# GpSimd's order in the local-attention stage of a hybrid decoder block: gate-weight sums ahead of the softmax denominators, in an order set by hand

## The chip, the cores and the metric

The kernel runs on one core of one Trainium2 chip. The metric is the device time of one execution in microseconds (us), the median of several runs; lower is better.

## What is computed

One residual block of a decoder with two attention mixers side by side and a SwiGLU, on 1024 tokens of width 1024, all in float32. The part that matters here:

```python
h = rmsnorm(x, mix_norm_g[l])
proj = h @ w_in[l]
qa, ka, va, q_lat, kv_lat, k_r, g_a, g_b = jnp.split(proj, IN_OFFSETS, axis=-1)
...
o_a = swa_sink_attention(qa, ka, va, swa_sinks[l])     # 8 heads, 2 kv heads, window 128
...
o_b = mla_attention(q_nope, q_rope, k_nope, k_rope, vb)
y = jax.nn.sigmoid(g_a) * (o_a @ w_o_swa[l]) + jax.nn.sigmoid(g_b) * (o_b @ w_o_mla[l])
x = x + y @ w_out[l]
h = rmsnorm(x, ffn_norm_g[l])
x = x + (jax.nn.silu(h @ w_gate[l]) * (h @ w_up[l])) @ w_down[l]
```

and in the local attention, per block of 128 queries against 256 keys:

```python
m = jnp.maximum(jnp.max(s, axis=-1, keepdims=True), sink)
p = jnp.exp(s - m)
denom = jnp.sum(p, axis=-1, keepdims=True) + jnp.exp(sink - m)
p = (p / denom).astype(v.dtype)
o = jnp.einsum('bnhgqk,bnkhd->bnqhgd', p, vw)
```

## The kernel before

Every float32 product is made of three products of halves: `split` (L159) lets ScalarE cast an operand to its upper half (L163) and VectorE subtract that from it for the lower half (L166); `mm3` (L168) multiplies upper by upper (L172), upper by lower (L173) and lower by upper (L174).

The stage around the change computes two independent things at once.

*The gate projections*, h @ [g_a | g_b], are most of TensorE's work. They go in eight column groups j, and each group is made of seven block products instead of eight (`Seven`), numbered q and run in the order 1, 6, 2, 7, 5, 4, 3. One `gate_step` (L850) runs one block product, twelve matmuls of 128x512. `run` (L789) first prepares the operand of the step two ahead (`prep`, L764), which means a split of a weight block `wr`, or of a sum `sm` for q = 6 and 5. The sums of the next group are made by `mix` (L750) when the step with q = 5 runs. On GpSimd these are six operations of 128x256, three for each half of the columns: sm0 = a21 + a22 (L180), sm1 = sm0 - a11 (L177) and a21 = a11 - a21 (L177). The weights have been scaled by the norm's gain on ScalarE before (L837). For q = 7 `prep` also subtracts sm1 from a12 in place, two GpSimd operations (L774, in the profile L177 wr<-wr,sm), after the split of a12 for q = 2 has read it.

*Local attention* goes in 16 iterations `it`, each one group of four heads and one block of 128 queries. Iteration `it` of the loop (L1025) issues, in this order: the load of queries two ahead (`sw_q`), gate step 3*it, the transposes of the next queries (`sw_qT`, L896), gate step 3*it+1, the product of probabilities and values of the iteration before (`sw_pv`), the scores of the next iteration (`sw_scores`, L905), gate step 3*it+2, and the transposes of its own probabilities (`sw_pT`, L950). Inside `sw_scores`, VectorE adds the band mask and takes row maxima (L921), joins them with the sinks (nm, L925; es, L927); ScalarE takes the exponentials and their row sums (pe, den, L933); GpSimd adds the sink's term (L935), takes the reciprocal as a power of -1 (L936) and scales the four heads' probabilities (L938).

With seven block products to a group and three steps to an iteration, the place of the sums moves through the loop: they fall to the steps 4, 11, 18, 25, 32, 39 and 46, and the subtractions from a12 to the steps 1, 8, 15, 22, 29, 36, 43 and 50.

What sets the order: TensorE and SyncE (SP, which issues all the DMAs here) run in the order in which the code is written (L335). ScalarE, VectorE and GpSimd are put in order by the framework's scheduler in this stage, since their hand-set stretch (L504) ends before the loop. Each engine works through its list strictly in that order, and waits at an instruction whose inputs aren't there. Tiles of the pools `U` (21 buffers), `V`, and `tiny` (8 buffers of each width) rotate, so an instruction that writes a new tile also waits for the last reader of the buffer's former one.

Of the kernel before, what the change touches and what calls it, by code (L numbers as in the profile page):

```python
# [12 lines left out]
ALU = mybir.AluOpType  # L13
# [76 lines left out]
def hybrid_block_kernel(  # L90
# [29 lines left out]
    nc = tc.nc  # L120
# [23 lines left out]
    def U(name, dt=F32, shape=(P, 1024)):  # L144
        return pool.tile(list(shape), dt, tag="u", name=uid(name))
# [4 lines left out]
    def tiny(name, w=1):  # L150
        return small.tile([P, w], F32, tag=f"t{w}", name=uid(name))

    def P1(name, shape=(P, 512)):
        return ps1.tile(list(shape), F32, tag="ps", name=uid(name))

    def PX(name, shape=(P, 512)):
        return psum["x"].tile(list(shape), F32, tag="ps", name=uid(name))
# [24 lines left out]
    def blk(b, n=1):  # L182
        return slice(b * P, (b + n) * P)
# [10 lines left out]
    neg_one = const.tile([P, 4], F32, name="neg_one")  # L194
# [139 lines left out]
    engines = mybir.EngineType  # L334
# [486 lines left out]
    sw = {}  # L821
# [28 lines left out]
    def gate_step():  # L850
        late = gate_stores[:]
        gate_stores.clear()
        gates.run()
        for d, t in late:
            nc.sync.dma_start(d, t)
# [3 lines left out]
    def sw_q(it):  # L859
        qn = U("qn")  # L860
        nc.sync.dma_start(qn[:, 0:256], q_d[it])
        sw[it] = {"qn": qn}
# [28 lines left out]
    def sw_qT(it):  # L891
        d = sw[it]
        qn = d.pop("qn")
        ptq = PX("qT", (P, 2, P))
        for j in range(2):
            nc.tensor.transpose(ptq[:, j], qn[:, blk(j)], ident)  # L896
        qs = U("qs", F32R, (P, 2, 2, P))
        e, o = qs[:, :, 0], qs[:, :, 1]
        nc.scalar.copy(e[0:64], ptq[0:64])
        nc.scalar.copy(o[64:128], ptq[64:128])  # L900
        nc.vector.tensor_tensor(e[64:128], ptq[0:64], e[0:64].bitcast(F32), op=ALU.subtract)
        nc.vector.tensor_tensor(o[0:64], ptq[64:128], o[64:128].bitcast(F32), op=ALU.subtract)
        d["qs"] = qs

    def sw_scores(it):  # L905
        g, b = divmod(it, NB)
        d = sw[it]
        qs = d.pop("qs")
        c0 = P if b == 0 else 0
        kc = slice((b - 1) * P + c0, (b + 1) * P)  # L910
        mx = tiny("mx", 4)
        scs = []
        for hp in range(2):
            sc = PX("sc", (P, 2, 2 * P))
            scs.append(sc)
            for j in range(2):
                nc.tensor.matmul(sc[:, j, c0:], qs[:, hp, j], khd[g][0][:, kc], start=True, stop=False)
                nc.tensor.matmul(sc[:, j, c0:], qs[:, hp, j], khd[g][1][:, kc], start=False, stop=True)
            for j in range(2):
                h = 2 * hp + j  # L920
                nc.vector.tensor_tensor_reduce(sc[:, j, c0:], sc[:, j, c0:], band[:, c0:], 1.0, NEG, op0=ALU.add,  # L921
                                               op1=ALU.max, accum_out=mx[:, h:h + 1])
        ns = nsink[:, 4 * g:4 * g + 4]
        nm = tiny("nm", 4)
        nc.vector.scalar_tensor_tensor(nm, mx, -SC_A, ns, op0=ALU.mult, op1=ALU.min)  # L925
        es = tiny("es", 4)
        nc.vector.tensor_tensor(es, nm, ns, op=ALU.subtract)  # L927
        den = tiny("den", 4)
        pe = U("pe", F32, (P, 4, 2 * P))
        for h in range(4):  # L930
            if h == 1:
                nc.scalar.activation(es, es, AF.Exp)
            nc.scalar.activation(pe[:, h, c0:], scs[h // 2][:, h % 2, c0:], AF.Exp, scale=SC_A, bias=nm[:, h:h + 1],  # L933
                                 accum_out=den[:, h:h + 1])
        nc.gpsimd.tensor_tensor(den, den, es, op=ALU.add)  # L935
        nc.gpsimd.tensor_tensor(den, den, neg_one, op=ALU.pow)  # L936
        for h in range(4):
            nc.gpsimd.tensor_scalar(pe[:, h, c0:], pe[:, h, c0:], den[:, h:h + 1], 0.0, op0=ALU.mult, op1=ALU.add)  # L938
        d["pe"] = pe
        d["kbs"] = [1] if b == 0 else [0, 1]  # L940

    def sw_pT(it):
        d = sw[it]
        pe = d.pop("pe")
        d["pth"] = U("pth", F32R, (P, 2, 4, P))
        d["ptl"] = U("ptl", F32R, (P, 2, 4, P))
        for kb in d["kbs"]:
            pp = P1("pT", (P, 4, P))
            for h in range(4):
                nc.tensor.transpose(pp[:, h], pe[:, h, blk(kb)], ident)  # L950
            split(d["pth"][:, kb], d["ptl"][:, kb], pp)

    def sw_pv(it):
        g, b = divmod(it, NB)
        d = sw.pop(it)
        kbs = d["kbs"]
        po = P1("o", (P, 2, 2, P))
        for kb in kbs:
            kblk = b - 1 + kb
            vst = vv[kblk // 4][:, kblk % 4, g]  # L960
            nc.tensor.matmul(po, vst, d["pth"][:, kb], start=kb == kbs[0], stop=False)
            nc.tensor.matmul(po, vst, d["ptl"][:, kb], start=False, stop=kb == 1)
        tmp = U("ot", F32, (P, 2, 2, P))
        nc.scalar.copy(tmp[0:64], po[64:128])
        if b % 4 == 0:
            oa_t[it // 4] = U("oa", F32, (P, 2, 512))
        oa = oa_t[it // 4]
        oc = blk(b % 4)
        nc.vector.tensor_tensor(oa[0:64, :, oc], po[0:64, :, 0], tmp[0:64, :, 0], op=ALU.add)
        nc.vector.tensor_tensor(oa[64:128, :, oc], po[0:64, :, 1], tmp[0:64, :, 1], op=ALU.add)  # L970
        if b % 4 == 3:
            nc.sync.dma_start(oa_d[it // 4], oa_t.pop(it // 4))
# [6 lines left out]
    for i, b in enumerate((4, 5, 6, 7, 0, 1, 2, 3)):  # L979
        ps = P1("kl", (P, KVL))  # L980
        mm3(ps, [(hT(k, blk(b)), (wkl[k // 4][0][:, k % 4], wkl[k // 4][1][:, k % 4])) for k in range(NK)])
        t = U("lat", F32, (P, 2, KVL))
        nc.scalar.copy(t[:, 0], ps)
        ss = tiny("ss")
        nc.scalar.activation(t[:, 1], t[:, 0], AF.Square, accum_out=ss)
        r = rstd_of(ss, KVL)
        if i == 0:
            latent_end(NB - 1)
            sw_qT(0)
            while lat_out:  # L990
                lat_store()
        if i == 2:
            gates.prep_to(1)
        if i == 3:
            gates.mix(0, nc.vector)
        if i == 4:
            sw_scores(0)
            gates.prep_to(2)
        if i >= 4:
            t4_of_h(i - 4)  # L1000
        scaled.append((t, r, b))
        if i == 4:
            gates.load_part(1, 0)
        while len(scaled) > (2 if i < 5 else 1):
            kv_out(*scaled.pop(0))
# [12 lines left out]
    def load_lat(n):  # L1018
        for b in range(len(lat), n):
            t = U("lat", F32, (P, LAT))  # L1020
            nc.sync.dma_start(t, lat_d[b])
            lat.append(t)

    N_SW = 2 * NB
    for it in range(N_SW):  # L1025
        if it + 2 < N_SW:
            sw_q(it + 2)
        gate_step()
        if it + 1 < N_SW:
            sw_qT(it + 1)  # L1030
        gate_step()
        if it >= 1:
            sw_pv(it - 1)
        if it + 1 < N_SW:
            sw_scores(it + 1)
        if it == N_SW - 1:
            load_lat(4)
        gate_step()
        sw_pT(it)
    gate_step()  # L1040
    gate_step()
    sw_pv(N_SW - 1)
    in_order.__exit__(None, None, None)


# [314 lines left out]
    for t in range(NT):  # L1360
        h, n = divmod(t, NB)
# [16 lines left out]
        if t in fill:  # L1378
            dc, sh, c0 = fill[t]
# [505 lines left out]
```

## Time and profile before

| | us |
|---|---|
| median of 3 runs | 1340.86 |
| lowest and highest | 1339.17, 1341.85 |
| the profiled execution | 1340.2 |
| its span in the trace | 1338.4 |
| TensorE busy | 1325.0 |
| VectorE busy | 904.0 |
| ScalarE busy | 635.5 |
| GpSimd busy | 566.9 |

Local attention and most of the gate projections lie between about 128 and 330 us. In the profile's rows an instruction is named by engine (PE is TensorE, DVE VectorE, ACT ScalarE, POOL GpSimd), the line of the kernel, the operation, and the tiles that it writes and reads (out<-in). A timeline row begins with its start and its duration; "x4" means four like it in a row, and brackets hold the engine's idle time just before and what ended it. `wl` is a prepared weight operand, `pT` the transposes of probabilities, `qT` those of queries.

### The profile page before, as it was taken

Reading aid. Unit: us, or ns where it says so; the run is one execution under the profiler, and the core shown is the slowest. Engines: PE = TensorE matmul, PEld = TensorE weight load, DVE = VectorE, ACT = ScalarE, POOL = GpSimd, SP = SyncE. Lnnn points to the kernel's source line nnn. Section 1 sums busy time; section 2 is a strip of 40 time slices with the busy share of each in tenths; the row PEclk is TensorE's granted clock in tenths of the full one; section 3 lists DMA queues with packets and bytes.
Section 4 is the critical chain, followed back from the end, with each engine's and each line's share of the span. In section 5 each row is a group of like instructions: output and inputs, shape, how many; then the busy total and the mean of one; then the engine's idle time right before and its main releaser. Section 6 shows DMA issues by size and latency. Waiting matters only on the chain. (4 is left out here: it accounts for less than half of the span.)

```text
span 1338.4 us, 19037 instructions
## 1 busy us (share of the span) xinstructions
PE 1325.0 (99%) x6564; PEld 1115.5 (83%) x6564; DVE 904.0 (68%) x1471; ACT 635.5 (47%) x1291; POOL 566.9 (42%) x614
## 2 busy tenths in 40 slices
PE   9999999999999999999999999999999999999997
PEld 6899878888888889888887888888888888888886
DVE  7868777776767766696468766566655564664862
ACT  7434767665557666763436323222233232644443
POOL 2116546553224555451131765756666541022521
PEclk9999999999999999999999999999999999999999
DMA  9455332245476440681533344535543425996504
GB/s 370 158 184 160 114 104 84 100 134 178 161 235 174 95 111 17 240 281 61 212 139 104 144 173 171 198 143 182 181 147 144 170 100 193 386 367 238 173 15 143
DMA packets 85311, 223.61 MB, mean 167 GB/s; under 512 B 9632, under 2 KB 16288, under 8 KB 84128
## 3 DMA queue, kind: packets, MB, share of 16 engines
q1 hardware_dynamic: 83776, 220.05, 47.9%
q10 hardware_dynamic: 1440, 2.36, 0.5%
q8 instruction: 52, 0.85, 0.3%
q14 instruction: 43, 0.35, 0.1%
HBM read 151.72 MB, written 70.12 MB: 166 GB/s over the span
## 5 line engine op out<-in xcount | busy, mean ns | idle before, releaser
L166 DVE TENSOR_TENSOR wl<-wr,wl 128x512 fp32r<-128x512 f32 x150 | 149.3, 1019 | 72.0 <-ACT wl L163 71.7
L166 DVE TENSOR_TENSOR lrv<-lr,lrv 128x1024 fp32r<-128x1024 f32 x77 | 105.2, 1397 | 48.7 <-ACT lrv L163 44.6
L163 ACT CAST lrv<-lr 128x1024 fp32r<-128x1024 f32 x77 | 80.0, 1052 | 95.0 <-PE fd L174 70.1
L172 PE MATMUL fd<-lrv 128*128 128x512 f32 x308 | 119.8, 389 | 0.0
L173 PE MATMUL fd<-lrv 128*128 128x512 f32 x308 | 119.8, 389 | 0.0
L174 PE MATMUL fd<-lrv 128*128 128x512 f32 x308 | 119.8, 389 | 0.0
L177 POOL TENSOR_TENSOR wr<-wr,sm 128x512 f32<-128x512 f32 (+1 forms) x38 | 46.6, 1234 | 145.8 <-DVE wl L166 115.5
L163 ACT CAST wl<-wr 128x512 fp32r<-128x512 f32 x150 | 87.0, 623 | 1.8 <-DVE wr L835 1.5
L1198 POOL TENSOR_TENSOR denb<-denb,neg_one 128x1 f32<-128x1 f32 x64 | 40.1, 626 | 96.2 <-ACT p L1197 84.0
L166 DVE TENSOR_TENSOR wl<-sm,wl 128x512 fp32r<-128x512 f32 x60 | 49.0, 844 | 46.4 <-ACT wl L163 46.2
L173 PEld LDWEIGHTS fd<-lrv 128*128 128x128 f32 x308 | 57.8, 188 | 12.1
L172 PEld LDWEIGHTS fd<-lrv 128*128 128x128 f32 x308 | 57.8, 188 | 12.0
L174 PEld LDWEIGHTS fd<-lrv 128*128 128x128 f32 x308 | 57.8, 188 | 11.8
L311 POOL TENSOR_SCALAR ms<-ss 128x1 f32<-128x1 f32 x32 | 8.5, 266 | 138.1 <-ACT xn L1644 61.0
L1197 ACT ACTIVATE p<-scb,nmb 128x384 f32<-128x384 f32 (+3 forms) x64 | 47.8, 747 | 33.3 <-DVE nmb L1196 25.6
L166 DVE TENSOR_TENSOR ptl<-pTb,pth 128x512 fp32r<-128x512 f32 (+2 forms) x96 | 50.5, 552 | 16.6 <-ACT pth L163 16.3
L1196 DVE CUSTOM_DVE_ANT_0 scb<-scb,mask 128x384 f32<-128x384 f32 (+3 forms) x64 | 48.6, 762 | 15.0 <-PE scb L1188 13.0
L1529 ACT ACTIVATE act<-sm 128x512 f32<-128x512 f32 x11 | 7.0, 634 | 104.4 <-DVE sm L180 104.4
L1199 POOL TENSOR_SCALAR p<-p,denb 128x384 f32<-128x384 f32 (+3 forms) x64 | 47.9, 748 | 6.3
L1529 ACT ACTIVATE act<-pu 128x512 f32<-128x512 f32 x22 | 13.9, 633 | 70.8 <-DVE pu L180 70.8
L163 ACT CAST pth<-pTb 128x512 fp32r<-128x512 f32 (+2 forms) x96 | 43.4, 482 | 8.5 <-PE pTb L1213 7.5
L172 PE MATMUL fb<-t2h,wl 128*128 128x512 f32 x120 | 47.4, 395 | 0.0
(356 smaller groups left out, 4318.0 us busy)
## 6 DMA issues: line engine op xcount, KB each, us to landing
lr<-la_d SPq DMA_DIRECT2D x77, 256.0 KB, 5.4
wr<-in_w_gate_dram SPq DMA_DIRECT2D x22, 512.0 KB, 4.2
wr<-in_w_up_dram SPq DMA_DIRECT2D x22, 512.0 KB, 5.2
wd<-in_w_down_dram SPq DMA_DIRECT2D x22, 512.0 KB, 7.2
rb_d<-wd SPq DMA_DIRECT2D x22, 512.0 KB, 2.7
la_d<-sd SPq DMA_DIRECT2D x22, 512.0 KB, 5.7
lr<-rb_d SPq DMA_DIRECT2D x44, 256.0 KB, 5.4
lr<-in_w_down_dram SPq DMA_DIRECT2D x33, 256.0 KB, 5.2
```

What stands on the lines that cost most here:

```text
L163: i = nc.scalar.copy(hi, src)
L166: (eng or nc.vector).tensor_tensor(lo, src, hi.bitcast(F32), op=ALU.subtract)
L172: nc.tensor.matmul(ps, ah, bh, start=first and i == 0, stop=False, skip_group_check=go_on)
L173: nc.tensor.matmul(ps, ah, bl, start=False, stop=False, skip_group_check=go_on)
L174: nc.tensor.matmul(ps, al, bh, start=False, stop=last and i == n - 1, skip_group_check=go_on)
L177: eng.tensor_tensor(out, a, b, op=ALU.subtract)
L311: nc.gpsimd.tensor_scalar(ms, ss, 1.0 / width, EPS, op0=ALU.mult, op1=ALU.add)
L1196: nc.vector.tensor_tensor_reduce(s_, s_, m_, 1.0, -NEG, op0=ALU.add, op1=ALU.min, accum_out=nm)
L1197: nc.scalar.activation(p_, s_, AF.Exp, scale=-1.0, bias=nm, accum_out=den)
L1198: nc.gpsimd.tensor_tensor(den, den, neg_one[:, 0:1], op=ALU.pow)
L1199: nc.gpsimd.tensor_scalar(p[:, 0:w], p[:, 0:w], den, 0.0, op0=ALU.mult, op1=ALU.add)
L1529: nc.scalar.activation(dst, src, AF.Silu)
```

## The change

The two operations on denominators and the four scalings move out of `sw_scores` into a function `norm`, which the loop calls one iteration later in the program: for iteration `it` behind gate step 3*it and the transposes of the next queries. Around the loop GpSimd is put into the order in which the code is written.

```diff
-        nc.gpsimd.tensor_tensor(den, den, es, op=ALU.add)
-        nc.gpsimd.tensor_tensor(den, den, neg_one, op=ALU.pow)
-        for h in range(4):
-            nc.gpsimd.tensor_scalar(pe[:, h, c0:], pe[:, h, c0:], den[:, h:h + 1], 0.0, op0=ALU.mult, op1=ALU.add)
+
+        def norm():
+            nc.gpsimd.tensor_tensor(den, den, es, op=ALU.add)
+            nc.gpsimd.tensor_tensor(den, den, neg_one, op=ALU.pow)
+            for h in range(4):
+                nc.gpsimd.tensor_scalar(pe[:, h, c0:], pe[:, h, c0:], den[:, h:h + 1], 0.0, op0=ALU.mult, op1=ALU.add)
+
+        d["norm"] = norm
...
+    pool_order = tc.manual_schedule(engines={engines.Pool})
+    pool_order.__enter__()
     for it in range(N_SW):
         if it + 2 < N_SW:
             sw_q(it + 2)
         gate_step()
         if it + 1 < N_SW:
             sw_qT(it + 1)
+        sw[it].pop("norm")()
         gate_step()
...
     sw_pv(N_SW - 1)
+    pool_order.__exit__(None, None, None)
     in_order.__exit__(None, None, None)
```

In the built programs TensorE, VectorE, ScalarE and SyncE have their instructions in the same order as before; only GpSimd's list differs, and in iterations 4 to 6 and 11 to 13 alone, apart from the order of the six sums among themselves. Six of ScalarE's instructions (L933) and seven of VectorE's (mostly L927 and L969) get an explicit wait for GpSimd that was implied before by another one.

GpSimd's list at iteration 4, before the change. `den_2201` and `pe_2202` are that iteration's denominators and probabilities, `sm_2217` the sums of gate group 2 and `wr_2025`, `wr_2089` its weights:

```order
L938 TENSOR_SCALAR pe_2072<-pe_2072,den_2071 128x256 x4
L180 TENSOR_TENSOR sm_2217<-wr_2025,wr_2089 128x256
L935 TENSOR_TENSOR den_2201<-den_2201,es_2199 128x4
L180 TENSOR_TENSOR sm_2217<-wr_2025,wr_2089 128x256
L936 TENSOR_TENSOR den_2201<-den_2201,neg_one 128x4
L177 TENSOR_TENSOR sm_2217<-sm_2217,wr_2025 128x256
L938 TENSOR_SCALAR pe_2202<-pe_2202,den_2201 128x256 x4
L177 TENSOR_TENSOR wr_2025<-wr_2025 128x2x128
L177 TENSOR_TENSOR sm_2217<-sm_2217,wr_2025 128x256
L177 TENSOR_TENSOR wr_2025<-wr_2025 128x2x128
```

The same place on GpSimd with the change, where the numbers of the tiles and the lines differ (`den_2203`, `pe_2204`, `sm_2213`, `wr_2027`, `wr_2085`; L937 to L940 stand for L935 to L938):

```order
L940 TENSOR_SCALAR pe_2074<-pe_2074,den_2073 128x256 x4
L180 TENSOR_TENSOR sm_2213<-wr_2027,wr_2085 128x256
L177 TENSOR_TENSOR sm_2213<-sm_2213,wr_2027 128x256
L177 TENSOR_TENSOR wr_2027<-wr_2027 128x2x128
L180 TENSOR_TENSOR sm_2213<-wr_2027,wr_2085 128x256
L177 TENSOR_TENSOR sm_2213<-sm_2213,wr_2027 128x256
L177 TENSOR_TENSOR wr_2027<-wr_2027 128x2x128
L937 TENSOR_TENSOR den_2203<-den_2203,es_2201 128x4
L938 TENSOR_TENSOR den_2203<-den_2203,neg_one 128x4
L940 TENSOR_SCALAR pe_2204<-pe_2204,den_2203 128x256 x4
```

The denominators and scalings stood among the six sums and now stand behind them. Iteration 11 reads alike.

GpSimd's list at iterations 5 and 6, before the change. `den_2328` and `den_2459` are the denominators of these iterations, `wr_2089` (subtracting `sm_2217`) is the pair for a12 of gate group 2, and `sm_2514` are the sums of group 3:

```order
L935 TENSOR_TENSOR den_2328<-den_2328,es_2326 128x4
L936 TENSOR_TENSOR den_2328<-den_2328,neg_one 128x4
L938 TENSOR_SCALAR pe_2329<-pe_2329,den_2328 128x256 x4
L177 TENSOR_TENSOR wr_2089<-wr_2089,sm_2217 128x2x128 x2
L935 TENSOR_TENSOR den_2459<-den_2459,es_2457 128x4
L936 TENSOR_TENSOR den_2459<-den_2459,neg_one 128x4
L938 TENSOR_SCALAR pe_2460<-pe_2460,den_2459 128x256 x4
L180 TENSOR_TENSOR sm_2514<-wr_2344,wr_2385 128x256 x2
L177 TENSOR_TENSOR sm_2514<-sm_2514,wr_2344 128x256
```

The same place on GpSimd with the change (`den_2330`, `den_2461`, `wr_2085` and `sm_2510` are the same tiles under new numbers):

```order
L177 TENSOR_TENSOR wr_2085<-wr_2085,sm_2213 128x2x128 x2
L937 TENSOR_TENSOR den_2330<-den_2330,es_2328 128x4
L938 TENSOR_TENSOR den_2330<-den_2330,neg_one 128x4
L940 TENSOR_SCALAR pe_2331<-pe_2331,den_2330 128x256 x4
L180 TENSOR_TENSOR sm_2510<-wr_2340,wr_2381 128x256
L177 TENSOR_TENSOR sm_2510<-sm_2510,wr_2340 128x256
L177 TENSOR_TENSOR wr_2340<-wr_2340 128x2x128
L180 TENSOR_TENSOR sm_2510<-wr_2340,wr_2381 128x256
L177 TENSOR_TENSOR sm_2510<-sm_2510,wr_2340 128x256
L177 TENSOR_TENSOR wr_2340<-wr_2340 128x2x128
L937 TENSOR_TENSOR den_2461<-den_2461,es_2459 128x4
```

The pair for a12 moved ahead of iteration 5's denominators, and the six sums ahead of iteration 6's. Iterations 12 and 13 read alike.

## The prediction

> **What bounds the kernel now.** I read the page first. Its first part says which engine is full:
>
> ```profile
> PE 1325.0 (99%) x6564; PEld 1115.5 (83%) x6564; DVE 904.0 (68%) x1471; ACT 635.5 (47%) x1291; POOL 566.9 (42%) x614
> ```
>
> TensorE (PE) is busy for 1325.0 of 1338.4 us, so nothing that is done on GpSimd (POOL) counts unless TensorE stands still for it. The next view is therefore what TensorE itself waited for, cut to the stretch in which local attention runs (128 to 330 us), and then the timeline of its probability transposes (pT), one group per iteration:
>
> ```profile
> PE fa L172 <- ACT wl L163: 1.9, 2, 1.1
> ...
> 181.33 1.03 PE L950 MATMUL pT<-ident,pe 128*128 128x128 f32 x8
> 192.54 1.03 PE L950 MATMUL pT<-ident,pe 128*128 128x128 f32 x8
> 205.49 1.03 PE L950 MATMUL pT<-ident,pe 128*128 128x128 f32 x8
> ...
> 271.89 1.03 PE L950 MATMUL pT<-ident,pe 128*128 128x128 f32 x8
> 284.53 1.03 PE L950 MATMUL pT<-ident,pe 128*128 128x128 f32 x8
> ```
>
> The first row says that TensorE waited twice here, 1.9 us in all, each time for a ScalarE (ACT) cast of gate weights. The start times give the full price. From 181.33 to 192.54 is 11.21 us, an undisturbed iteration. From 192.54 to 205.49 is 12.95, and from 271.89 to 284.53 is 12.64, for the same work. These are the intervals behind iterations 4 and 11 of 0 to 15. The losses are 1.74 and 1.43 us, **3.17 us together**. They exceed the 1.9 us because TensorE also restarts slowly:
>
> ```profile
> 196.15 0.38 PE L896 MATMUL qT<-ident,qn 128*128 128x128 f32 x2
> ...
> 197.61 0.50 PE L172 MATMUL fa<-hh,wl 128*128 128x512 f32 x1 [1.08 <-ACT wl L163]
> ...
> 198.34 0.50 PE L174 MATMUL fa<-hh,wl 128*128 128x512 f32 x1
> 198.67 0.40 PE L172 MATMUL fa<-hh,wl 128*128 128x512 f32 x1
> 198.91 0.40 PE L173 MATMUL fa<-hl,wl 128*128 128x512 f32 x1
> ```
>
> The three products that start from 197.61 took until 198.67, 1.06 us, where the next one took 0.24 (198.67 to 198.91). The third (L174) multiplies by the lower half of the weights, which comes from VectorE (DVE) after the cast.
>
> Who made that cast late is read backwards, first on ScalarE, then VectorE, then GpSimd. The figure in brackets is the idle time before a row and what ended it.
>
> ```profile
> 175.70 1.71 ACT L837 ACTIVATE wr<-wr,gT 128x256 f32<-128x256 f32 x4
> 190.25 0.62 ACT L163 CAST wl<-sm 128x512 fp32r<-128x512 f32 x1 [4.10 <-POOL sm L177]
> 195.03 0.48 ACT L933 ACTIVATE pe<-sc,nm 128x256 f32<-128x256 f32 x1 [3.67 <-DVE nm L925]
> 196.93 0.63 ACT L163 CAST wl<-wr 128x512 fp32r<-128x512 f32 x1
> ...
> 188.19 0.43 DVE L902 TENSOR_TENSOR qs<-qT,qs 64x256 fp32r<-64x256 f32 x1
> 190.91 0.69 DVE L166 TENSOR_TENSOR wl<-sm,wl 128x512 fp32r<-128x512 f32 x1 [2.29 <-ACT wl L163]
> 195.03 0.16 DVE L927 TENSOR_TENSOR es<-nm,nsink 128x4 f32<-128x4 f32 x1
> 197.59 0.69 DVE L166 TENSOR_TENSOR wl<-wr,wl 128x512 fp32r<-128x512 f32 x1 [1.80 <-ACT wl L163]
> ...
> 176.69 0.74 POOL L180 TENSOR_TENSOR sm<-wr,wr 128x256 f32<-128x256 f32 x1 [0.95 <-ACT wr L837]
> 183.53 0.20 POOL L935 TENSOR_TENSOR den<-den,es 128x4 f32<-128x4 f32 x1 [6.10 <-ACT pe L933]
> 183.68 0.74 POOL L180 TENSOR_TENSOR sm<-wr,wr 128x256 f32<-128x256 f32 x1
> 185.82 0.74 POOL L177 TENSOR_TENSOR sm<-sm,wr 128x256 f32<-128x256 f32 x1
> 186.54 2.27 POOL L938 TENSOR_SCALAR pe<-pe,den 128x256 f32<-128x256 f32 x4
> 189.48 0.74 POOL L177 TENSOR_TENSOR sm<-sm,wr 128x256 f32<-128x256 f32 x1
> ...
> 269.31 0.62 ACT L163 CAST wl<-sm 128x512 fp32r<-128x512 f32 x1 [3.81 <-POOL sm L177]
> ```
>
> The late cast is wl<-wr at 196.93. It stands on ScalarE behind the exponentials, which began at 195.03 after 3.67 us of waiting for VectorE; VectorE was late because wl<-sm at 190.91 came late; and that waited for ScalarE's cast of the sums at 190.25, which had waited 4.10 us for GpSimd. GpSimd had begun the six sums at 176.69, but its second operation was the denominators of iteration 4 (183.53), for which it sat idle 6.10 us, and the last sum that is needed ran at 189.48, behind the four scalings at 186.54. Iteration 11 repeats this: 3.81 us before 269.31. So the wait that TensorE pays at 197.61 begins 14 us earlier, with one GpSimd instruction (183.53) that stands ahead of the sums and isn't ready.
>
> **The change part by part.** No work is added or removed: 16 times two operations on denominators and four scalings, seven times six sums, eight pairs of subtractions, as before. What moves is order on one engine. It issues no DMA, and SP, ScalarE, VectorE and TensorE keep their order.
>
> *Iterations 4 and 11: sums ahead.* The inputs of the sums are scaled by ScalarE at 175.70 to 177.41, all four pieces. From 176.69 six sums of 0.74 us end at about 181.1, before the exponentials of iteration 4 let the denominators start at 183.53. The denominators lose nothing. The cast of the sums can go when ScalarE is free, 190.25-4.10 = 186.15. VectorE is free at 188.62 (188.19+0.43) instead of waiting to 190.91, so its chain from there to es at 195.03 moves up by 2.29 us; the exponentials begin at 192.74, the critical cast runs 194.64 to 195.27, its lower half 195.30 to 195.99. TensorE comes for the upper half behind qT, at 196.15+0.38 = 196.53 at the latest, and for the lower half two products (0.46) later. Both are there about 1 us early (195.27 for 196.53, 195.99 for 196.99). Gain 1.74 us, and 1.43 us in iteration 11: **3.17 us**.
>
> *Iterations 5 and 12: the subtraction from a12 (two operations) ahead of the denominators. Iterations 6 and 13: six sums ahead.* These rows show what is queued behind, and when TensorE comes for it:
>
> ```profile
> 197.13 0.20 POOL L935 TENSOR_TENSOR den<-den,es 128x4 f32<-128x4 f32 x1 [6.21 <-ACT pe L933]
> 198.52 1.84 POOL L938 TENSOR_SCALAR pe<-pe,den 128x256 f32<-128x256 f32 x4
> 200.32 1.86 POOL L177 TENSOR_TENSOR wr<-wr,sm 128x256 f32<-128x256 f32 x2
> 207.75 0.20 POOL L935 TENSOR_TENSOR den<-den,es 128x4 f32<-128x4 f32 x1 [5.56 <-ACT pe L933]
> 209.14 2.37 POOL L938 TENSOR_SCALAR pe<-pe,den 128x256 f32<-128x256 f32 x4
> ...
> 203.06 1.71 ACT L837 ACTIVATE wr<-wr,gT 128x256 f32<-128x256 f32 x4
> ...
> 216.70 1.03 PE L950 MATMUL pT<-ident,pe 128*128 128x128 f32 x8
> ```
>
> The pair (200.32, 1.86 us) must wait for VectorE's lower half of the same weights, by the above 196.0, so it runs to 197.9; denominators and scalings (1.39 us from 197.13 to 198.52, then 1.84 to 2.37) end near 201.6, where they ended at 200.36. TensorE transposes them at 205.49-1.74 = 203.75: 2.1 us to spare. The sums of iteration 6 wait for the scaled weights of 203.06 to 204.77, some 2 us earlier now, and for the scalings; they end near 206.6, the denominators follow to 210.4, and TensorE comes at 216.70-1.74 = 214.96. Cost nothing; if the cover were gone, each us beyond it would be a us of TensorE, and the transposes stand ahead of all later gate products in its queue.
>
> *New waits.* Six first exponentials on ScalarE and seven VectorE instructions (es, oa, one wl) now wait for GpSimd by name, because a rotated buffer was last read there. What they name are denominators and scalings two iterations back, and an iteration is 11.21 us. Behind each stands its engine's whole queue, but at that age the price is nothing.
>
> *What the trace doesn't show* is sums running while VectorE makes the row maxima final. GpSimd was always waiting then. Now sums overlap nm and es (the maxima's sign and the sinks, both short) in iterations 6 and 13, and reach up to them in 4 and 11. Nearest rows:
>
> ```profile
> 184.00 0.97 DVE L166 TENSOR_TENSOR wl<-wr,wl 128x512 fp32r<-128x512 f32 x1 [1.78 <-ACT wl L163]
> 208.21 0.69 DVE L166 TENSOR_TENSOR wl<-wr,wl 128x512 fp32r<-128x512 f32 x1 [1.76 <-ACT wl L163]
> 205.45 0.16 DVE L925 SCALAR_TENSOR_TENSOR nm<-mx,nsink 128x4 f32<-128x4 f32 x1
> ...
> 209.23 0.48 PE L172 MATMUL fb<-t4h,wl 128*128 128x512 f32 x1
> ```
>
> The subtraction that makes a lower half took 0.97 us beside a GpSimd sum (184.00) and 0.69 without one (208.21): such an overlap costs 0.3 us. For nm and es the bounds are nothing and one sum each, 2 x 0.74 = 1.48 us. The lower half ends at 208.90 and is wanted two products (0.46) behind 209.23, at 209.69, so 0.8 us are free: a loss of 0 to 0.7 us per place, 0 to 1.4 in all. A gain is excluded, since GpSimd was idle beside them. I take nothing, since 2 x 0.3 us, by the nearest row, fits into the 0.8.
>
> [...]
>
> *Carrying it to the end.* Time saved in mid-kernel is only kept if TensorE stays the bound. These two windows (bounds, length, then TensorE busy) say it does:
>
> ```profile
> 330.00:390.00 60.00, 60.00 (x281) 49.59 (x280) 38.19 (x65) 28.13 (x54) 12.44 (x12) 1.00 0.63 211
> 722.00:1115.00 393.00, 393.00 (x1734) 325.49 (x1735) 252.47 (x310) 117.18 (x215) 227.73 (x158) 1.00 0.45 160
> ```
>
> The sum against the profiled execution is 1340.2-3.2 = 1337.0 us. That execution lies 0.7 us under the median of the three runs (1340.86), so the forecast for the median is **1337.7 us**.
>
> **The rivals.** *Both stalls go* (forecast): 1337.7. For it: the sums' inputs are there by 177.41, 6 us before the place that held them.
>
> *The saving is partly taken back*, by sums that delay nm and es in iterations 6 and 13, or because the cast of iterations 4 and 11 turns out tighter than my 1 us. Against it: one overlap was seen to cost 0.3 us. With it, 0.5 to 1.6 us of the 3.2 return (the 1.4 above, and 0.2 for a tighter cast): 1338.2 to 1339.3, at its likeliest 1339. [...]
>
> *The change doesn't do what it says*: ScalarE's late exponentials have another cause, for instance VectorE's own backlog, and both waits remain: 1340.9. Against it: VectorE idled before 190.91, and ScalarE before 190.25, both behind that sum.
>
> *Slower, by late probabilities.* In strict order the subtraction of iterations 5 and 12 holds denominators and scalings behind VectorE. If GpSimd ended them later than 203.75, TensorE would stand at pT, twice. The spare 2.1 us is the point from which it decides. If both old stalls still go, a net loss of 2.7 us needs (3.2+2.7)/2 = 2.9 us beyond that at each place, 5.0 us in all; even a pair of twice its 1.86 us would bring 1.9. It would then be about 1344.
>
> **How the numbers follow.** A measurement of this kernel tells about 0.2%, 2.7 us, from no change, and the forecast gain of 3.2 lies only just beyond it. Chances: both stalls go 0.66, partly back 0.23, no effect 0.06, slower 0.05. The first case lands a little under the bound now and then (0.08), and the second once in ten beyond it, so faster 0.60, same 0.35, slower 0.05. The three runs before lie from 1.7 below their median to 1.0 above it. So the range goes from 1337.7-1.7 = 1336.0 to the partial case's upper bound and the same spread, 1339.3+1.0 = 1340.3; it leaves out no effect and slower.
>
> **What would show it.** Right: iterations 4 and 11 take 11.21 us from pT to pT like the rest, TensorE's wait for the cast of wl is gone between 128 and 330 us, and GpSimd's six sums stand in one run from about 176.7 to 181. The scalings of iteration 5 then end about 2 us before their transposes. Wrong: nm or es longer than 0.16 us in iterations 6 and 13 with a wait of TensorE some 4 us later (partly back); an idle time before pT with GpSimd as releaser (slower); or a wait that moved to another engine ahead of 196.9.

## The result, and the profile after

The changed kernel took 1338.30 us (median of 22 runs, 1336.31 to 1340.04) against 1340.78 us of the kernel before beside it (22 runs). The two medians differ by 2.5 us; the ratio, worked out over all these runs, is 0.9976, which is 3.2 us less, with a 95% interval of 0.9969 to 0.9983, 2.3 to 4.2 us. 1337.7 was predicted, 1336.0 to 1340.3 as the range. The profiled execution took 1336.93 us with a span of 1335.1; the span of before was 1338.4, 3.3 us more.

What TensorE waited for between 128 and 330 us is an empty answer now: the row of the cast (1.9 us, 2 times) is gone and no other has come. TensorE's busy time is the page's first part again; then the starts of the probability transposes, from its timeline:

```profile
PE 1323.6 (99%) x6564; PEld 1115.3 (84%) x6564; DVE 904.6 (68%) x1471; ACT 636.5 (48%) x1291; POOL 567.0 (42%) x614
```

```profile
180.87 1.03 PE L954 MATMUL pT<-ident,pe 128*128 128x128 f32 x8
192.08 1.03 PE L954 MATMUL pT<-ident,pe 128*128 128x128 f32 x8
203.29 1.03 PE L954 MATMUL pT<-ident,pe 128*128 128x128 f32 x8
...
269.69 1.03 PE L954 MATMUL pT<-ident,pe 128*128 128x128 f32 x8
280.91 1.03 PE L954 MATMUL pT<-ident,pe 128*128 128x128 f32 x8
```

192.08 to 203.29 is 11.21 us where 12.95 stood, and 269.69 to 280.91 is 11.22 where 12.64 stood. From the first transposes of the loop to the last, sixteen groups, it is 147.88 to 313.29 = 165.41 us against 148.37 to 316.91 = 168.54: **3.13 us saved**, all of it in these two intervals. The profiled execution also began its loop 0.49 us earlier, ahead of anything that the change touches, so times of the two traces are compared as distances from a transposition and not as they stand.

Behind the next query transposes of iteration 4, the gate products now run without a gap: the first starts at 195.83, and from the second on one follows every 0.23 to 0.24 us:

```profile
195.69 0.38 PE L896 MATMUL qT<-ident,qn 128*128 128x128 f32 x2
195.83 0.48 PE L172 MATMUL fa<-hh,wl 128*128 128x512 f32 x1
196.14 0.40 PE L173 MATMUL fa<-hl,wl 128*128 128x512 f32 x1
196.38 0.40 PE L174 MATMUL fa<-hh,wl 128*128 128x512 f32 x1
196.61 0.40 PE L172 MATMUL fa<-hh,wl 128*128 128x512 f32 x1
```

The chain that led there, in GpSimd's, ScalarE's and VectorE's timelines of the changed kernel:

```profile
176.23 0.74 POOL L180 TENSOR_TENSOR sm<-wr,wr 128x256 f32<-128x256 f32 x1 [0.95 <-ACT wr L837]
...
179.96 0.73 POOL L177 TENSOR_TENSOR wr<-wr 128x256 f32<-128x256 f32 x1
183.19 0.20 POOL L937 TENSOR_TENSOR den<-den,es 128x4 f32<-128x4 f32 x1 [2.50 <-ACT pe L933]
...
195.19 1.44 POOL L177 TENSOR_TENSOR wr<-wr,sm 128x256 f32<-128x256 f32 x2 [8.24 <-DVE wl L166]
196.59 0.20 POOL L937 TENSOR_TENSOR den<-den,es 128x4 f32<-128x4 f32 x1
196.87 1.51 POOL L938 TENSOR_TENSOR den<-den,neg_one 128x4 f32<-128x4 f32 x1
198.47 2.36 POOL L940 TENSOR_SCALAR pe<-pe,den 128x256 f32<-128x256 f32 x4
201.26 0.74 POOL L180 TENSOR_TENSOR sm<-wr,wr 128x256 f32<-128x256 f32 x1 [0.43 <-ACT wr L837]
...
202.77 0.74 POOL L177 TENSOR_TENSOR wr<-wr 128x256 f32<-128x256 f32 x1
203.47 0.73 POOL L180 TENSOR_TENSOR sm<-wr,wr 128x256 f32<-128x256 f32 x1
...
204.97 0.74 POOL L177 TENSOR_TENSOR wr<-wr 128x256 f32<-128x256 f32 x1
205.90 0.20 POOL L937 TENSOR_TENSOR den<-den,es 128x4 f32<-128x4 f32 x1 [0.19 <-ACT pe L933]
...
207.29 2.36 POOL L940 TENSOR_SCALAR pe<-pe,den 128x256 f32<-128x256 f32 x4
```

```profile
185.77 0.62 ACT L163 CAST wl<-sm 128x512 fp32r<-128x512 f32 x1
...
191.84 0.47 ACT L933 ACTIVATE pe<-sc,nm 128x256 f32<-128x256 f32 x1 [2.69 <-DVE nm L925]
...
193.75 0.63 ACT L163 CAST wl<-wr 128x512 fp32r<-128x512 f32 x1
...
203.61 0.47 ACT L933 ACTIVATE pe<-sc,nm 128x256 f32<-128x256 f32 x1 [1.63 <-POOL wr L177]
```

```profile
187.69 0.69 DVE L166 TENSOR_TENSOR wl<-sm,wl 128x512 fp32r<-128x512 f32 x1
...
191.84 0.16 DVE L927 TENSOR_TENSOR es<-nm,nsink 128x4 f32<-128x4 f32 x1
...
194.41 0.69 DVE L166 TENSOR_TENSOR wl<-wr,wl 128x512 fp32r<-128x512 f32 x1 [1.44 <-ACT wl L163]
...
202.86 0.67 DVE L925 SCALAR_TENSOR_TENSOR nm<-mx,nsink 128x4 f32<-128x4 f32 x1
203.56 0.65 DVE L927 TENSOR_TENSOR es<-nm,nsink 128x4 f32<-128x4 f32 x1
...
206.36 0.69 DVE L166 TENSOR_TENSOR wl<-wr,wl 128x512 fp32r<-128x512 f32 x1 [1.55 <-ACT wl L163]
```

The six sums run in one piece from 176.23 to 180.69, and the denominators of iteration 4 still start at 183.19. ScalarE casts the sums at 185.77 with no wait in brackets, VectorE follows at 187.69, its es stands at 191.84 instead of 195.03, and the cast that TensorE had waited for starts at 193.75 instead of 196.93. It ends 1.45 us before the first product that needs it (194.38 for 195.83), and VectorE's lower half 1.28 us before the third (195.10 for 196.38). The scalings of iteration 5 end at 200.83, 2.46 us ahead of 203.29. One thing is new: nm and es of iteration 6 (202.86 and 203.56) took 0.67 and 0.65 us, each while a sum ran on GpSimd. The same two of iteration 13 took 0.67 and 0.58; in the kernel before neither took more than 0.17 anywhere in the loop. In iterations 2, 4 and 11 the last sum now ends inside nm, which took 0.28 to 0.30 there. (The exponential at 203.61 names the sum that ended at 203.51, but it also needs nm, which ended at 203.53; for iteration 13 the profile names nm.)

### The profile page after: what moved, and what is told of

Its sections match the earlier page's. It is cut to its first block, busy times and chain, and to the rows that moved or that the text cites. A ratio compares the mean times of both kernels' runs of the same rounds, so it can differ in the third digit from the quotient of the medians.

```text
span 1335.1 us, 19045 instructions
## 1 busy us (share of the span) xinstructions
PE 1323.6 (99%) x6564; PEld 1115.3 (84%) x6564; DVE 904.6 (68%) x1471; ACT 636.5 (48%) x1291; POOL 567.0 (42%) x614
## 5 line engine op out<-in xcount | busy, mean ns | idle before, releaser
L166 DVE TENSOR_TENSOR wl<-wr,wl 128x512 fp32r<-128x512 f32 x150 | 148.7, 1015 | 71.2 <-ACT wl L163 70.9
L166 DVE TENSOR_TENSOR lrv<-lr,lrv 128x1024 fp32r<-128x1024 f32 x77 | 105.1, 1396 | 49.0 <-ACT lrv L163 46.4
L166 DVE TENSOR_TENSOR wl<-sm,wl 128x512 fp32r<-128x512 f32 x60 | 48.2, 829 | 42.2 <-ACT wl L163 42.1
L172 PEld LDWEIGHTS fd<-lrv 128*128 128x128 f32 x308 | 57.8, 188 | 11.9
L166 DVE TENSOR_TENSOR ptl<-pTb,pth 128x512 fp32r<-128x512 f32 (+2 forms) x96 | 50.5, 551 | 16.6 <-ACT pth L163 16.2
```

The source lines that it names most:

```text
L166: (eng or nc.vector).tensor_tensor(lo, src, hi.bitcast(F32), op=ALU.subtract)
L172: nc.tensor.matmul(ps, ah, bh, start=first and i == 0, stop=False, skip_group_check=go_on)
```

## The experiments

The intervals below are differences of the starts of neighbouring groups of probability transposes, behind the iteration named; all others are 11.2 us in all kernels, save those behind iteration 0 (10.3 to 11.9, ahead of the change's first effect), 8 and 14 (10.3 and 10.0 everywhere). Ratios are to the kernel before, run beside each.

| kernel | behind 4 | 5 | 11 | 12 | ratio (95%) |
|---|---|---|---|---|---|
| before | 12.95 | 11.21 | 12.64 | 11.21 | 1 |
| the change | 11.21 | 11.22 | 11.22 | 11.21 | 0.9976 (0.9969 to 0.9983) |
| only sums ahead in 4, 11 | 11.23 | 11.23 | 11.22 | 11.23 | 0.9973 (0.9964 to 0.9981) |
| sums behind | 13.75 | 11.23 | 13.48 | 11.22 | 1.0017 (1.0008 to 1.0026) |
| all but those sums | 15.19 | 11.21 | 14.93 | 11.22 | 1.0032 (1.0021 to 1.0043) |
| two more powers | 11.21 | 11.22 | 11.21 | 11.21 | 0.9975 (0.9966 to 0.9984) |
| four more powers | 11.80 | 12.30 | 11.80 | 12.34 | 1.0002 (0.9994 to 1.0011) |
| two-input ops beside sums | 11.21 | 11.66 | 11.21 | 11.65 | 0.9984 (0.9975 to 0.9992) |
| two-input ops alone | 11.22 | 11.23 | 11.22 | 11.23 | 0.9978 (0.9969 to 0.9986) |
| one-input ops beside sums | 11.23 | 11.67 | 11.23 | 11.66 | 0.9989 (0.9981 to 0.9998) |

*Which part brings the gain.* The change has three parts that can be had one by one, since a denominator function called at its old place stays ahead of the sums and the pair. The next three kernels differ from the changed one only in that:

```diff
-        d["norm"] = norm
+        if it in (3, 4, 10, 11):
+            d["norm"] = norm
+        else:
+            norm()
...
-        sw[it].pop("norm")()
+        if "norm" in sw[it]:
+            sw[it].pop("norm")()
```

With this condition only the sums of 4 and 11 go ahead:

> Only one part of the change: the sums of iterations 4 and 11 stand ahead of the denominators; the pairs of iterations 5 and 12 and the sums of 6 and 13 stand where they stood before. My theory: the whole gain, 3.2 us below before (ratio 0.9976), 11.21 us from pT to pT in every full iteration; nm and es of iterations 6 and 13 back at 0.16 us each (0.67 and 0.65 in the changed kernel). Rival (the pairs and the later sums carry part of the gain): a gain clearly under 3 us, with an interval over 11.5 us left behind iteration 4, 5, 6, 11, 12 or 13.

It has the whole gain, 0.9973, and every interval at 11.2. nm and es of iteration 6 are short again, in VectorE's timeline of this kernel:

```profile
203.80 0.16 DVE L925 SCALAR_TENSOR_TENSOR nm<-mx,nsink 128x4 f32<-128x4 f32 x1
204.00 0.16 DVE L927 TENSOR_TENSOR es<-nm,nsink 128x4 f32<-128x4 f32 x1
...
206.62 0.69 DVE L166 TENSOR_TENSOR wl<-wr,wl 128x512 fp32r<-128x512 f32 x1 [1.42 <-ACT wl L163]
```

So the other two parts of the change bring nothing. With the condition `it in (3, 10)` GpSimd's order is also set by hand, but the sums of 4 and 11 stand wholly behind:

> GpSimd's order set by hand as in the change, but in iterations 4 and 11 the six sums stand wholly behind the denominators and scalings, and iterations 5, 6, 12, 13 are as before the change. My theory (only the sums' place counts): in the changed kernel the denominators of iteration 4 ran at 183.19 and its scalings ended at 186.95; five sums of 0.74 us behind them end near 190.6, 0.4 us later than the 190.22 of before, so both stalls stay and grow by about 0.4 us each: pT to pT 13.3 and 13.0 us, all told 0.8 us above the kernel before (ratio 1.0006). Rival (an order by hand at all, or the explicit waits, brings the gain): about 3 us below before, ratio 0.998, and 11.21 us from pT to pT throughout.

The stalls stayed and grew, to 2.53 and 2.26 us over 11.22; a hand-set order alone gains nothing. They grew by 0.80 and 0.84, twice what was expected: that estimate set a time of the changed kernel's trace against one of before without taking off the 0.49 us between their starts. TensorE's waits between 128 and 330 us, and the fifth sum on GpSimd with the cast that it releases on ScalarE:

```profile
PE fa L172 <- ACT wl L163: 3.2, 2, 1.6
```

```profile
190.15 0.74 POOL L177 TENSOR_TENSOR sm<-sm,wr 128x256 f32<-128x256 f32 x1
```

```profile
190.92 0.62 ACT L163 CAST wl<-sm 128x512 fp32r<-128x512 f32 x1 [4.89 <-POOL sm L177]
```

The third condition, `it not in (4, 11)`, is the rest of the change without its first part:

> The rest of the change without its first part: the pairs of iterations 5 and 12 ahead of the denominators and the sums of 6 and 13 ahead of theirs, but the sums of 4 and 11 behind. My theory: as with the sums behind and nothing else changed, about 0.8 us above before (ratio 1.0006), pT to pT 13.3 and 13.0 us behind iterations 4 and 11, the rest 11.21. Two places shift against each other here: with the stall back, VectorE's lower half of the pair's weights is late, so the pair and with it the denominators of iteration 5 come about 2 us later, but TensorE comes later by the stall too. Rival (the later parts carry gain): below before by 1 us or more.

No gain, as expected, but 15.19 and 14.93 us instead of 13.3 and 13.0. The wait was no longer than with the sums behind alone (3.2 us in two waits in both). What came on top is in the windows of the trace (bounds, length, busy time of the five engines, then TensorE's granted clock) and in TensorE's timeline:

```profile
198.00:200.00 2.00, 1.35 (x4) 0.84 (x5) 1.37 (x3) 2.00 (x6) 0.60 (x1) 0.92 0.96 347
200.00:203.00 3.00, 3.00 (x8) 2.32 (x8) 2.91 (x6) 2.93 (x8) 2.82 (x5) 0.50 0.46 177
```

```profile
198.65 0.53 PE L172 MATMUL fa<-hh,wl 128*128 128x512 f32 x1 [1.59 <-ACT wl L163]
...
199.75 0.63 PE L172 MATMUL fa<-hh,wl 128*128 128x512 f32 x1
200.18 0.63 PE L173 MATMUL fa<-hl,wl 128*128 128x512 f32 x1
```

After the stall the granted clock was 0.50, and products started 0.43 us apart instead of 0.23, until 203.1. Whether the pairs or the later sums bring this on, or chance, took four more kernels on one chip: sums behind and the pairs of 5 and 12 ahead (`it in (3, 5, 10, 12)`), sums behind and only the later sums ahead (`it in (3, 6, 10, 13)`), and both kernels from above again.

> Sums of iterations 4 and 11 behind the denominators as in the run with the sums behind, and in addition the pairs of 5 and 12 ahead of the denominators as in the change; sums of 6 and 13 behind theirs. That run was at 1.0017 of before with stalls of 2.53 and 2.26 us; with the pairs and the later sums ahead as well it was 1.0032, and after both stalls TensorE's granted clock was 0.50 for some 3.5 us (200 to 203 us), which made each interval 1.44 longer. If the drop of the clock is a matter of chance after a stall of 1.6 us, it comes in some executions of this kernel and of the other three here, whatever GpSimd's order: the same mix of mean clocks from 0.996 to 0.999 and times of about 1342 without a drop, 1343.5 with one, 1345 with two. If the pair ahead brings it on: near 1.0032, clock 0.996 to 0.997 in most runs, unlike the kernel without it.

> Sums of iterations 4 and 11 behind the denominators, pairs of 5 and 12 behind them too, and only the sums of 6 and 13 ahead of theirs. If the drop of the clock is chance: intervals behind iterations 4 and 11 of about 13.7 and 13.5 us, or 1.45 more where a drop falls, and a ratio between 1.0010 and 1.0035 like the others. If the sums of 6 and 13 ahead cost time by themselves (the nm and es held beside them, 1.0 us per place): intervals behind iterations 5, 6, 12 or 13 above 11.3 us, and up to 1.1 us above the run with the sums behind.

> The kernel with the sums behind and nothing else, once more, beside the other three on one chip. Without a drop of the clock, 2.5 and 2.3 us at the two places, against 1.74 and 1.43 before: 1.6 us above before (ratio 1.0012). If the drop is chance, some of its runs have a mean clock of 0.997 or less and are 1.45 us longer per drop, the profiled one perhaps too.

> The kernel with everything but the first part of the change, once more, on the same chip. If the drop is chance, its median moves towards that of the kernel with the sums behind (ratio 1.0012 to 1.0035), and the profiled execution may have none, with intervals of 13.7 and 13.5 us behind iterations 4 and 11. If the order of the pairs and the later sums brings the drop on, it stays at about 1.0032 with two drops in the profile and clocks of 0.996, 1.5 us or more above the kernel with the sums behind.

| kernel | behind 4 | behind 11 | ratio (95%) | runs with a mean clock of 0.996 |
|---|---|---|---|---|
| pairs ahead | 15.17 | 13.34 | 1.0025 (1.0016 to 1.0033) | 3 of 11 |
| later sums ahead | 13.75 | 13.47 | 1.0020 (1.0012 to 1.0029) | 1 of 11 |
| sums behind again | 13.73 | 13.45 | 1.0023 (1.0013 to 1.0032) | 3 of 10 |
| all but those sums again | 13.63 | 13.32 | 1.0020 (1.0011 to 1.0029) | 3 of 11 |

In the six profiles of these kernels here and above, two drops go with a mean clock of 0.996, one with 0.997, and none with 0.998 or 0.999; that is how the last column is read. The four intervals of the ratio overlap. Behind iterations 5, 6, 12 and 13 the kernel with only the later sums ahead shows 11.2 us, so those sums cost nothing by themselves. With the pairs ahead one drop came, behind iteration 4 alone. The kernel with all but those sums had two in its first profile and none in the second, whose window from 200 to 203 us reads:

```profile
200.00:203.00 3.00, 3.00 (x17) 2.54 (x16) 2.91 (x6) 2.94 (x8) 2.82 (x4) 1.00 0.49 195
```

So the order of the pairs doesn't decide it; the drop comes by execution, though 4 of 7 runs at 0.996 against 0 of 11 had suggested otherwise in the first comparison. What brings it on in one execution and not in the next stays open. Over the 61 executions of these kernels there and here, the 14 with a mean clock of 0.996 had a median of 1345.8 us, the 34 with 0.998 or 0.999 one of 1343.1. A drop lengthened its interval by some 1.5 us (15.19 against 13.63 for one kernel, 14.93 against 13.32).

*How much the late scalings may cost.* In iterations 5 and 12 of the changed kernel, more work was put ahead of the scalings, at first two reciprocals:

```diff
+            for _ in range(2 if it in (5, 12) else 0):
+                nc.gpsimd.tensor_tensor(den, den, neg_one, op=ALU.pow)
             nc.gpsimd.tensor_tensor(den, den, neg_one, op=ALU.pow)
```

> The changed kernel with two more reciprocals of the denominators (each undoes the other) on GpSimd in iterations 5 and 12, ahead of the scalings. In the changed kernel the scalings of iteration 5 ended at 200.83 and TensorE began the transposes at 203.29: 2.46 us spare. Two reciprocals of 1.02 us and their gaps are about 2.2 us. My theory (the spare time is a true cushion): 0 to 0.2 us lost per place, the time that of the changed kernel (ratio to before 0.9976 to 0.998), 11.21 us from pT to pT within 0.2. Rival (the wait is tighter than it looks, because queues or write latency take part of the spare time): 1 us or more lost at each place, and TensorE idle before pT.

No loss. GpSimd's last scaling and TensorE's transposes in this kernel:

```profile
201.83 1.84 POOL L942 TENSOR_SCALAR pe<-pe,den 128x256 f32<-128x256 f32 x4
```

```profile
203.94 1.03 PE L956 MATMUL pT<-ident,pe 128*128 128x128 f32 x8
```

The scalings ended at 203.67, 0.27 us ahead of 203.94. With `range(4 ...)` instead:

> The changed kernel with four more reciprocals of the denominators (in pairs that undo each other) on GpSimd in iterations 5 and 12, about 4.3 us more ahead of the scalings, whose last ended 2.46 us before the transposes began. The first group of transposes wants all four heads within about 0.4 us of its start, so the scalings would be late by 4.3-2.46-0.4 = about 1.4 us. My theory (each us beyond the spare time is a us of TensorE, as the slower rival of the prediction priced it): 1.4 to 2 us lost at each of two places, 3 to 4 us above the changed kernel, so about the time of the kernel before (ratio 0.9999 to 1.0006), with TensorE idle before pT and GpSimd named. Rival (TensorE has other work to hide it): no loss. Rival (the delay passes on to iterations 6 and 13 as well): above 5 us.

The two places lost 0.59 + 1.08 and 0.59 + 1.13 us, 3.4 in all, as the theory had it, and the ratio went to 1.0002. TensorE stood ahead of the transposes, and the eight then took 2.12 us where 1.03 is usual, while GpSimd scaled the four heads until 206.87:

```profile
205.56 2.12 PE L956 MATMUL pT<-ident,pe 128*128 128x128 f32 x8 [0.42 <-POOL pe L942]
```

```profile
205.03 1.84 POOL L942 TENSOR_SCALAR pe<-pe,den 128x256 f32<-128x256 f32 x4
```

*Why nm and es are longer beside the sums.* Two VectorE instructions of the same size, both inputs in SBUF, were put ahead of nm in iterations 6 and 13 of the changed kernel:

```diff
+        for _ in range(2 if it in (6, 13) else 0):
+            nc.vector.tensor_tensor(mx, mx, mx, op=ALU.max)
```

> The changed kernel with two more VectorE instructions of 128x4 in iterations 6 and 13 just ahead of nm, the maximum of mx with itself: two inputs, both in SBUF. In the changed kernel nm and es took 0.67 and 0.65 us there beside GpSimd's sums and 0.16 elsewhere, and the lower half of the next weights was ready 0.44 us before TensorE wanted it. My theory (each such instruction is held for most of one sum): the two take about 0.67 each, the exponentials start 1.3 us later, the lower half comes 0.9 us too late, and TensorE loses 0.9 to 1.3 us at each place: 1.8 to 2.6 us above the changed kernel, ratio to before 0.9989 to 0.9996. Rival (nm and es were long for a reason of their own, not the sums): the two take 0.16 each, 0.3 us fits into the 0.44, no loss.

The same edit in the kernel that has only the sums of 4 and 11 ahead:

> The same two VectorE instructions ahead of nm in iterations 6 and 13, but in the version whose sums there stand behind the denominators, so that GpSimd does nothing beside them. My theory: the two, nm and es all take 0.16 us, the exponentials start 0.3 us later than without them and the lower half is about 0.6 us early: no loss, the time of the changed kernel (ratio to before 0.9976). Rival (two more instructions in this chain cost TensorE by themselves): the same loss as with the sums beside them.

And one input instead of two (`tensor_scalar(mx, mx, 1.0, None, op0=ALU.mult)`), in the changed kernel:

> As with the maximum of mx with itself beside the sums, but the two added instructions multiply mx by 1: one input. [...] If any small VectorE instruction is held beside a sum, they take about 0.67 each and the loss is 1.8 to 2.6 us, as with two inputs.

VectorE's timelines at iteration 6: the two-input instructions beside the sums, then alone, then the one-input instructions beside the sums ("x2" stands for both):

```profile
203.13 1.36 DVE L926 TENSOR_TENSOR mx<-mx 128x4 f32<-128x4 f32 x2
204.52 0.16 DVE L927 SCALAR_TENSOR_TENSOR nm<-mx,nsink 128x4 f32<-128x4 f32 x1
204.72 0.59 DVE L929 TENSOR_TENSOR es<-nm,nsink 128x4 f32<-128x4 f32 x1
207.46 0.69 DVE L166 TENSOR_TENSOR wl<-wr,wl 128x512 fp32r<-128x512 f32 x1 [1.55 <-ACT wl L163]
```

```profile
203.41 0.36 DVE L926 TENSOR_TENSOR mx<-mx 128x4 f32<-128x4 f32 x2
```

```profile
205.38 1.37 DVE L926 TENSOR_SCALAR mx<-mx 128x4 f32<-128x4 f32 x2
206.79 0.16 DVE L927 SCALAR_TENSOR_TENSOR nm<-mx,nsink 128x4 f32<-128x4 f32 x1
```

1.36 us beside the sums, 0.36 alone: the sums hold them. The loss was 0.45 and 0.44 us at the two places, half of what was expected, because of the four small instructions the third, nm, took 0.16 us: it began at 204.52, in the gap between two sums (204.47 to 204.54). The lower half came 4.59 us behind the transposes' start (208.15 and 203.56) against 3.76 in the changed kernel (207.05 and 203.29): 0.83 later where 0.54 were free, so 0.29 too late, and the rest of the loss went into TensorE's restart, as at iteration 4 before (again 1.06 us for the three products, 207.48 to 208.54, against 0.78 in the changed kernel, 207.04 to 207.82). Alone they cost nothing. With one input it was 1.37 us, 0.68 for each instruction, as expected for the case that any small one is held, and the same loss of 0.44 to 0.45.

## Why the prediction was right, step by step

*The two stalls, 3.17 us.* Measured 3.13 in the intervals, and the run with only these sums ahead shows that they carry all of it. The chain was read rightly: the sums behind brought back each wait, 0.8 us longer, for a last sum that came 0.7 us later (190.15 instead of 189.48). Between 188.19 and es VectorE's chain moved by 3.19 us, or 2.70 with the earlier start taken off, against 2.29 predicted. Most of the rest comes from two lower halves ahead of it, at 184.00 and 186.09, that had run beside the sums before: they took 0.97 and 1.01 us there and take 0.69 and 0.68 now (183.66 and 185.47). The prediction didn't count this gain. It is more than needed, and TensorE stays the bound (busy for 1323.6 of 1335.1 us).

*The pair ahead in 5 and 12.* Predicted 2.1 us to spare, measured 2.46 in the trace. The two doses confirm it from both sides: with two more powers 0.27 us were left and nothing was lost, with four more, 1.7 us per place. The rival of late probabilities had the right place and about the right price, a microsecond of TensorE for a microsecond beyond: with four more powers the scalings ended 1.9 us behind the start that undisturbed transposes would have had (206.87 for 193.76 + 11.21 = 204.97). Its point of decision was not reached.

*The sums ahead in 6 and 13, nm and es.* This was the term without a row of its own, bounded by 0 and 1.48 us per place, with 0.6 taken as the likelier delay out of 0.8 free. Each of the two instructions was held for 0.5 us, not 0.3. The step that was off is the reading of the nearest row as a price per overlap. What it shows is the rest of a sum: the lower half at 184.00 began 0.42 us before its sum ended (183.68 + 0.74 = 184.42) and lost 0.28; nm began 0.65 before the end of its sum and lost 0.51, es 0.64 and lost 0.49. Each lost the rest of the sum less about 0.14. On ScalarE only part of it counts, since es is needed one exponential later than nm: behind the transposes' start the lower half came 0.68 us later than in the kernel with only the sums of 4 and 11 ahead (3.76 against 207.31 - 204.23 = 3.08, its transposes standing at 204.23). There 1.23 us were free (207.31 for the third product at 208.54), not the 0.8 of the prediction, so 0.54 remained (207.05 for 207.59). The cost to TensorE is nothing, as predicted, but with two sizes off: the delay on VectorE was 1.0 and not 0.6, the spare time 1.23 and not 0.8. Neither was known when the term was set at nothing, so that it came out at nothing was in part luck. Of the signs of being wrong that the prediction named for this case, the long nm and es appeared and the wait of TensorE did not. The upper bound of 1.48 us per place, one sum for each of the two, was the author's estimate and did not come up: it was 1.0 on VectorE (0.16 became 0.67 and 0.65) and 0.68 at the weights.

*The new waits* cost nothing: no row of TensorE's waits is left, and all fifteen intervals of the loop are as long as undisturbed ones were before.

*The median.* The forecast was 1337.7, the median came to 1338.3, and the saving is 2.5 us by the medians, 3.2 by the ratio, against 3.13 in the profile. The interval, 2.3 to 4.2 us, holds all three; nothing in the runs tells this 0.6 us from scatter.

## What to carry to other kernels

On an engine that works through its queue in order, ask of each instruction that waits long what stands behind it and was ready: here 0.2 us of work that idled 6.1 us held back sums whose lateness TensorE paid for 14 us later, by way of ScalarE and VectorE. A part of a reordering that ends no stall gained nothing here, and it used up spare time elsewhere: putting only those sums ahead gave the same time as the whole change and left the short VectorE instructions free of GpSimd. Check a margin that a trace shows by a dose at that place, one below it and one above: here 2.2 us of added work against a margin of 2.46 cost nothing, and 4.4 us cost 1.7 per place. When an overlap lengthens an instruction, ask what was left of the other one when it began, before taking the difference as a fixed price: here 0.42 us left of a sum cost 0.28, and 0.65 cost 0.51.

## What the runs showed of the hardware

*nm, es and the lower halves of weights, all with two inputs in SBUF, took longer where they began beside a GpSimd sum.* 0.16 us became 0.67 where a sum of 0.74 had just begun, and the ends coincide (203.53 for nm, 203.51 for the sum that began at 202.77). The lower half at 184.00, with 0.42 us left of its sum, took 0.97 instead of 0.69. In the traces of the kernels before and after, between 128 and 330 us, 26 of them (18 lower halves, L166 wl, six nm and two es) began at least 0.15 us before the end of a sum; each lost the rest of that sum less 0.13 to 0.14 us. The mask additions (L921), with one input in SBUF and one in PSUM, did not: in the changed kernel they took 0.41 to 0.43 us where they started beside the sums (201.38, 201.81 and 202.34), as they did before with GpSimd idle (203.97 to 204.92). The one-input instructions of the last experiment, from SBUF to SBUF, took as long beside the sums as those with two (1.37 and 1.36 us for a pair; alone, only the pair with two inputs was run, 0.36). So the number of inputs in SBUF doesn't tell the two kinds apart here, and what does was not shown.

*A stall of 1.6 us cost another 1.5 us in one execution, and not in another.* In the kernel with all but the sums of 4 and 11 ahead, TensorE's granted clock was 0.50 from 200 to 203 us behind a wait of 1.59 us, and products started 0.43 us apart for about 3.4 us (199.75 to 203.13); in the second profiled execution, whose longest wait was 1.6 us too, it was 1.00 there. In the kernel before, whose first wait of the kind was 1.08 us, the profile has 1.00 behind both.
